# A list scheduler that knows of the port between VectorE and GpSimd

## The chip, the cores and the metric

One core of a Trainium2 chip runs the whole program. The metric is the time of one execution on the device in microseconds (us), the median of three runs. Beside the runs one execution was recorded by the hardware profiler. The engines are TensorE (PE: products; PEld: its weight loads), VectorE (DVE), ScalarE (ACT), GpSimd (POOL) and SyncE (SP), which issues the loads.

## The reference

Two layers over 256 latent tokens and 256 context tokens of 1024 channels, all in float32. Layer 0 mixes tokens by a gated DeltaNet that runs forward and backward, layer 1 by differential attention; a SwiGLU follows each. Every sub-layer is modulated by shift, scale and gate vectors (adaLN) and closed by a LayerNorm.

```
for i in range(DEPTH):                                  # 2
    sh1, sc1, gt1, sh2, sc2, gt2 = split(s_lat @ ada_w[i] + ada_b[i])     # the same for the context
    h, hc = x * (1 + sc1) + sh1, ctx * (1 + sc1c) + sh1c
    y, yc = _gated_deltanet(h, hc, ...) if i == 0 else _diff_attention(h, hc, ...)
    x = _layernorm(DEEPNORM_ALPHA * x + gt1 * y, ln1_g[i], ln1_b[i])
    x = _layernorm(DEEPNORM_ALPHA * x + gt2 * _swiglu(x * (1 + sc2) + sh2, ...), ln2_g[i], ln2_b[i])
    # and the context in the same way, but in the last layer
return x
```

## The kernel before, in words

The order of nearly all instructions is not written by hand. The kernel is a set of generators, called threads: one loads the weights, one splits them, eight groups of nine work through the DeltaNet heads, one (dense_run) goes through the large products, others do the norms, the attention heads and the adaLN vectors. A thread yields operations (Op), each with an engine and an estimated cost, and Sched.run asks each thread when its next operation could start: when its engine is free by the estimates (at), when the thread's last operation has ended plus a delay between the two engines (LAG), and when other engines have left the same PSUM bank. The one that can start first is issued; among equals the thread of the lower rank. An Alt holds the same operation for several engines, and the one that would end first is taken, where spare adds a delay to VectorE's bid. So the estimates decide two things: the order on every engine's own queue, which the hardware then keeps, and which engine an Alt goes to. On the chip the instructions wait for each other by semaphores; the estimates are no longer used there.

TensorE's products take float32 operands as two parts of a narrower type, hi and lo, and mm3 adds three products of them. For the weights ScalarE casts the hi part (wh, wxh, wyh) and VectorE or GpSimd subtracts it from the weight, which gives the lo part (wl, wxl, wyl; lo_op, split). In stage A below lo_op goes to GpSimd unless that is later by 1e6 ns, afterwards by 1e3 ns. The activations' parts are hh and hl, those of the hidden channels hidh and hidl or h1h and h1l; q and k of attention are split into qs, ks and kl after a rotation (rope) that uses rs.

Where TensorE is idle by the estimates for at least 1000 ns, warm inserts products of the tile ones that nobody reads: one for each 216 ns of the wait but its last 600. In the profile they are the line L514 of before, and in what follows they are called fillers.

The stages in the order of time:

- A: the heads of the DeltaNet. Projections (pj), convolution (acc, cv), the inverse of a triangular matrix on small tiles (t) by VectorE, the scan, and the first part of the out-projection. The lo parts here, a sum of each convolution and the decay masks (PQ, EG) are on GpSimd.
- B: the rest of the out-projection, and the first norm (n, bst; sm holds its small vectors, rsqrt is a chain of small VectorE operations on them).
- C: SwiGLU of layer 0 (wgu, wd). Beside it VectorE sums adaLN vectors of later stages (adaE, ada_dve), which TensorE then transposes in the midst of the products.
- D: attention of layer 1. A head's output is normed by another rsqrt chain and ends in ao, which TensorE transposes.
- E: the last norm ahead of SwiGLU of layer 1, that SwiGLU, and the output's norm.

The norms' rows are scaled on GpSimd too (lnr; ln_x), as is in part the split of their results (hl).

Of the kernel before, what the change touches and what calls it, by code (L numbers as in the profile page):

```python
# [17 lines left out]
P = 128  # L18
# [8 lines left out]
# columns of the constants' array  # L27
# [22 lines left out]
def last(ap, n):  # L50
    """[P, a] -> [P, a, n], each value repeated."""
    return ap.unsqueeze(2).to_broadcast([ap.shape[0], ap.shape[1], n])


def mid(ap, n):
    """[P, b] -> [P, n, b], the row repeated."""
    return ap.unsqueeze(1).to_broadcast([ap.shape[0], n, ap.shape[1]])
# [17 lines left out]
# numbers of buffers  # L75
# [40 lines left out]
# The kernel is written as threads of operations. Each step issues the operation that can start first by an  # L116
# estimate of the engines' times; among equals, that of the thread with the lower rank. A thread's operations
# follow each other; threads meet at events and at the buffers they allocate and free.
class Op:
    __slots__ = ("eng", "cost", "fn", "wait", "banks")  # L120

    def __init__(self, eng, cost, fn, *aps):
        self.eng, self.cost, self.fn = eng, cost, fn
        # engines take turns at a bank of PSUM
        self.banks = {a.tensor.name for a in aps if a.space == PSUM}
        self.wait = 0.0     # the delay that is accepted to leave this engine to others


class Alt(list):
    """the same operation on several engines; the one that ends first is taken"""  # L130


class Par(list):
    """operations that do not depend on each other"""
# [10 lines left out]
class Tag:  # L145
    """buffers of one size. Tags of other types may share them; without a pool, a tag only counts"""
# [20 lines left out]
class Alloc:  # L167
    def __init__(self, *tags):
        # (a list may grow while the thread waits)
# [18 lines left out]
class Buf:  # L188
    """an allocated buffer; t is the tile"""
# [21 lines left out]
class Sched:  # L211
    # from the end of an operation to the start of another one that needs it
# [7 lines left out]
    def __init__(self):  # L220
        self.at = {"pe": 0.0, "v": 0.0, "s": 0.0, "g": 0.0, "dma": 0.0}
        self.threads = []
        self.banks = {}
        self.now = 0.0
# [16 lines left out]
    def advance(self, th):  # L241
        """run the thread to its next operation"""
# [47 lines left out]
    def start(self, th):  # L290
        """(start, end, operation) of the thread's next operation, or None while it waits"""
# [8 lines left out]
        for op in it if isinstance(it, Alt) else (it,):  # L300
            s = max(self.at[op.eng], base + self.lag(eng, op.eng))
            for b in op.banks:
# [7 lines left out]
    def run(self, until=None):  # L310
        while self.threads and not (until is not None and until.time is not None):
# [17 lines left out]
            if op.eng != "pe":  # L329
                # an operation of a lower rank that is about to come is worth a short wait  # L330
# [14 lines left out]
            self.at[op.eng] = e  # L345
            for b in op.banks:
                self.banks.setdefault(b, {})[op.eng] = e
# [10 lines left out]
def trunk_kernel(ctx: ExitStack, tc: tile.TileContext, A: dict, out: bass.AP, dbg=None, stop=None):  # L358
# [10 lines left out]
    # ------------------------------------------------------------ operations with their estimated cost  # L369
# [16 lines left out]

    def tt(o, a, b, op, e="v"):
        return Op(e, cost(e, o, (a, b)), lambda: E[e].tensor_tensor(o, a, b, op), o, a, b)  # L388
# [4 lines left out]
    def ts(o, a, s1, s2, o0, o1=None, e="v"):  # L393
        f = lambda: E[e].tensor_scalar(o, a, s1, s2, o0, o1) if o1 is not None else E[e].tensor_scalar(o, a, s1, s2, o0)  # L394
        return Op(e, cost(e, o, (a,), (s1, s2), True), f, o, a)

    def stt(o, a, s, b, o0, o1):
        return Op("v", cost("v", o, (a, b), (s,)), lambda: V.scalar_tensor_tensor(o, a, s, b, o0, o1), o, a, b)  # L398

    def cp(o, a, e="s"):  # L400
        if e == "s":
            return Op("s", cost("s", o, (a,)), lambda: S.copy(o, a), o, a)  # L402
        return Op(e, cost(e, o, (a,), (), True), lambda: E[e].tensor_copy(o, a), o, a)
# [13 lines left out]
    def spare(alt, wait):  # L417
        """leaves DVE free unless the others are later by this much"""
# [8 lines left out]
    def mm(o, l, r, start=True, stop=True):  # L427
        n, m = fs(r), fs(l)
        if l.dtype == F32R:
            c = max(n, 256) / 2.4 + 2  # L430
# [15 lines left out]
    def mm3(o, l, r, start, stop):  # L446
        """the three products of (hi, lo) operands that float32 accuracy needs"""
# [6 lines left out]
    # ranks: a lower one goes first  # L454
# [6 lines left out]
    # ------------------------------------------------------------ buffers of the whole run  # L461
    PS = {k: Tag(ps, [P, 512], F32, k, n) for k, n in (("pj", 2), ("wa", 2), ("wb", 1), ("wc", 2), ("o", 1))}
    YP = [PS[k] for k in ("wb", "wc", "o")]
    # weights: as they come, and their two parts
# [39 lines left out]
    def warm(a, b):  # L504
        """keeps TensorE's clock up while it waits from a to b: products that nobody reads, in a free bank"""
# [20 lines left out]
    def prep_s():  # L526
# [8 lines left out]
        # selB[:, r, :]: ones in the rows 32 g + r  # L535
# [4 lines left out]
    def rsqrt(x, n):  # L540
        """1/sqrt(x[:, :n]), x positive: a first guess from the bits, then two steps. Frees nothing of x"""
# [7 lines left out]
        # 8/3 of a step of third order, then one of second order  # L549
# [10 lines left out]
    # ------------------------------------------------------------ weights  # L560
    pieces = []   # (kind, key, source) in the order of their use
# [28 lines left out]
    def split(raw, n, hi, lo, e, loaded):  # L590
        """the part that float32r holds, and the rest"""
# [15 lines left out]
    def unit(w, i):  # L607
        """i-th quarter (512 columns) of the halves of a piece"""
# [7 lines left out]
    # ------------------------------------------------------------ adaLN vectors  # L616
    def ada_mm(l, v, hf, tag):
        """s @ W of 512 columns, in four row groups that remain to be summed"""
# [16 lines left out]
    def ada_mod_post(l, v, hf, pt):  # L635
        """mods[:, 4 hf.., r] = (s @ W + b [+ 1]) with channels on partitions; r = 0 latent, 1 context"""
# [27 lines left out]
    def ada_dve(l, v, hf, streams, post):  # L664
        """s @ W of 512 columns by DVE, the rows' products remain to be summed over the partitions"""
# [38 lines left out]
    def gate_out(l, v, hf, parts):  # L704
        """the gates, broadcast over the partitions: sums of rows that lhs selects"""
# [35 lines left out]
    # ================================================================= layer 0: gated DeltaNet  # L741
# [48 lines left out]
    # ---- decay and write gates of all heads  # L790
# [1396 lines left out]
```

## Time and profile before

| | before |
|---|---|
| runs, us | 1452.04, 1455.54, 1456.51; median 1455.54 |
| span of the profiled execution, us | 1456.0 |
| PE busy, us | 1282.4 (88%) |
| weight loads busy, us | 1044.1 (72%) |
| DVE busy, us | 1044.6 (72%) |
| ACT busy, us | 578.5 (40%) |
| POOL busy, us | 505.7 (35%) |
| mean granted clock of TensorE | 0.945 |
| DMA | 171.48 MB, 118 GB/s in the mean |

The profiled execution has no time of its own in the list; its span lies within the three runs. Busy time of an engine is the sum of its instructions' durations, and an instruction that stands on its engine waiting for something other than a semaphore counts as busy. The granted clock is the share of full speed that TensorE's throttle let through. Times within a stage are in us from the span's start.

### The profile page before, as it was taken

To read this page: it belongs to the slowest core of one execution; us is meant where nothing else is said; L and a number is where in the kernel's file an instruction comes from. 1 tells how busy PE (TensorE), PEld (TensorE's weight loads), DVE (VectorE), ACT (ScalarE), POOL (GpSimd) and SP (SyncE) were. 2 spreads that over 40 slices of the span, in tenths; PEclk is the share of its full clock that TensorE was granted. 3 is DMA by queue.
4 is the path that set the end of the run, shared out by engine and by line. 5 is a ranking of instruction groups with operands and counts; after the bars stand their busy time and mean duration, and the time that the engine had idled before them with its cause. 6 is when DMAs were issued, how large, how long until landed. Compare 5 with 4: busy or idle time off the path is not lost. (4 is left out here: it accounts for less than half of the span.)

```text
span 1456.0 us, 22451 instructions
## 1 busy us (share of the span) xinstructions
PE 1282.4 (88%) x8606; PEld 1044.1 (72%) x8606; DVE 1044.6 (72%) x2212; ACT 578.5 (40%) x1244; POOL 505.7 (35%) x315
## 2 busy tenths in 40 slices
PE   9977798786888987898999999998889978799997
PEld 6555566565667576877888777877777766799986
DVE  3488989989888558799448664256788878855546
ACT  2364565555553423322221222125445433444432
POOL 1166534445443144524211223226343332422200
PEclk9988999899899998999999999998899989899999
DMA  6524220100111342354425544221332224455551
GB/s 239 203 72 137 96 88 30 44 30 30 38 37 45 117 167 94 116 198 138 157 82 194 189 158 147 84 91 59 137 124 86 88 80 158 163 187 187 185 193 43
DMA packets 47196, 171.48 MB, mean 118 GB/s; under 512 B 5360, under 2 KB 5488, under 8 KB 46320
## 3 DMA queue, kind: packets, MB, share of 16 engines
q1 hardware_dynamic: 47088, 170.04, 34.0%
q8 instruction: 67, 1.10, 0.3%
q14 instruction: 41, 0.34, 0.1%
HBM read 168.97 MB, written 1.05 MB: 117 GB/s over the span
## 5 line engine op out<-in xcount | busy, mean ns | idle before, releaser
L437 PE MATMUL pj<-hl,wh 128*128 128x512 f32 (+1 forms) x648 | 239.7, 370 | 5.6 <-DVE hl L388 5.6
L437 PE MATMUL pj<-hh,wh 128*128 128x512 f32 (+1 forms) x648 | 239.0, 369 | 5.0 <-DVE w L398 1.8
L402 ACT CAST wh<-w 128x1024 fp32r<-128x1024 f32 (+1 forms) x136 | 141.7, 1047 | 224.8 <-PE wa L437 54.2
L388 POOL TENSOR_TENSOR wl<-w,wh 128x1024 fp32r<-128x1024 f32 (+1 forms) x53 | 130.2, 2459 | 266.9 <-ACT wh L402 242.0
L437 PE MATMUL pj<-hh,wl 128*128 128x512 f32 (+1 forms) x512 | 198.8, 388 | 0.0
L437 PEld LDWEIGHTS pj<-hh,wh 128*128 128x128 f32 x648 | 129.0, 199 | 22.2 <-issue 3.0
L437 PEld LDWEIGHTS pj<-hl,wh 128*128 128x128 f32 x648 | 128.7, 199 | 19.4 <-DVE hl L388 4.9
L398 DVE SCALAR_TENSOR_TENSOR adaE<-w,sT,adaE 128x512 f32<-128x512 f32 x112 | 110.8, 1023 | 10.1 <-DMA w<-in_adaw_dram 9.4
L388 DVE TENSOR_TENSOR t<-t,t 128x8 f32<-128x8 f32 (+14 forms) x240 | 114.1, 476 | 4.6
L437 PEld LDWEIGHTS pj<-hh,wl 128*128 128x128 f32 x512 | 102.4, 200 | 12.4
L437 PE MATMUL wa<-hh,wh 128*128 128x256 f32 (+2 forms) x312 | 102.7, 329 | 0.0
L437 PE MATMUL wa<-hl,wh 128*128 128x256 f32 (+2 forms) x312 | 102.7, 329 | 0.0
L388 DVE TENSOR_TENSOR wl<-w,wh 128x1024 fp32r<-128x1024 f32 x44 | 54.3, 1234 | 54.7 <-ACT wh L402 50.9
L388 POOL TENSOR_TENSOR acc<-acc,cv 128x508 f32<-128x508 f32 x48 | 64.2, 1341 | 53.2 <-ACT cv L415 50.2
L388 POOL TENSOR_TENSOR wxl<-w,wh 128x1024 fp32r<-128x1024 f32 x16 | 39.6, 2477 | 102.5 <-ACT wh L402 65.8
L388 POOL TENSOR_TENSOR h1l<-fth,h1h 128x256 fp32r<-128x256 f32 x22 | 32.1, 1457 | 99.2 <-ACT h1h L402 99.2
L437 PE MATMUL pj<-hh,wxl 128*128 128x256 f32 (+1 forms) x200 | 65.0, 325 | 0.0
L437 PEld LDWEIGHTS wa<-hh,wh 128*128 128x128 f32 (+1 forms) x312 | 60.3, 193 | 5.5
L437 PEld LDWEIGHTS wa<-hl,wh 128*128 128x128 f32 (+1 forms) x312 | 60.0, 192 | 5.5
L437 PE MATMUL wa<-hh,wxl 128*128 128x512 f32 (+1 forms) x176 | 61.6, 350 | 0.0
L437 PE MATMUL wa<-hh,wl 128*128 128x256 f32 (+2 forms) x176 | 58.0, 330 | 0.0
L402 ACT CAST wxh<-w 128x1024 fp32r<-128x1024 f32 x29 | 30.3, 1049 | 59.8 <-PE wa L437 21.4
(645 smaller groups left out, 3416.1 us busy)
## 6 DMA issues: line engine op xcount, KB each, us to landing
w<-in_adaw_dram SPq DMA_DIRECT2D x89, 512.0 KB, 4.3
w<-in_wgu_dram SPq DMA_DIRECT2D x64, 512.0 KB, 4.6
w<-in_wd_dram SPq DMA_DIRECT2D x36, 512.0 KB, 4.0
w<-in_wdn_dram SPq DMA_DIRECT2D x26, 512.0 KB, 3.7
wx<-in_wgu_dram SPq DMA_DIRECT2D x22, 512.0 KB, 4.8
w<-in_wo_dram SPq DMA_DIRECT2D x15, 512.0 KB, 3.8
w<-in_wqk_dram SPq DMA_DIRECT2D x12, 512.0 KB, 3.8
lnr<-in_lnr_dram SPq DMA_DIRECT2D x4, 1024.0 KB, 7.8
```

Source lines behind the costliest of these rows:

```text
L388: return Op(e, cost(e, o, (a, b)), lambda: E[e].tensor_tensor(o, a, b, op), o, a, b)
L398: return Op("v", cost("v", o, (a, b), (s,)), lambda: V.scalar_tensor_tensor(o, a, s, b, o0, o1), o, a, b)
L402: return Op("s", cost("s", o, (a,)), lambda: S.copy(o, a), o, a)
L437: return Op("pe", c, lambda: T.matmul(o, lhsT=l, rhs=r, start=start, stop=stop), o)
```

## The change

An Op gets a mark, port. It is set for every operation on GpSimd, and for one on VectorE when no source is in PSUM and it has two sources or writes to SBUF. The scheduler keeps for each of the two engines when its last marked operation ends, and lets a marked operation start, by the estimates, no earlier than the other engine's last one ends. Operations that are given as dve(...) (shuffles, transposes, reductions, statistics) are not marked. The estimate for a product of split operands goes from 1/2.4 ns a column plus 2 to 0.433 ns a column plus 8. Comments and docstrings go too, and the numbers of lines shift (L388 becomes L400, L437 L449, L441 L453, L514 L526).

```diff
 class Op:
-    __slots__ = ("eng", "cost", "fn", "wait", "banks")
+    __slots__ = ("eng", "cost", "fn", "wait", "banks", "port")
...
+        self.port = False
 class Sched:
...
+        self.port = {"v": 0.0, "g": 0.0}
     def start(self, th):
...
             s = max(self.at[op.eng], base + self.lag(eng, op.eng))
+            if op.port:
+                s = max(s, self.port["g" if op.eng == "v" else "v"])
     def run(self, until=None):
...
             self.at[op.eng] = e
+            if op.port:
+                self.port[op.eng] = e
...
+    def shared(op, srcs, out=None):
+        op.port = op.eng == "g" or (op.eng == "v" and not isps(*srcs) and (len(srcs) > 1 or not isps(out)))
+        return op
     def tt(o, a, b, op, e="v"):
-        return Op(e, cost(e, o, (a, b)), lambda: E[e].tensor_tensor(o, a, b, op), o, a, b)
+        return shared(Op(e, cost(e, o, (a, b)), lambda: E[e].tensor_tensor(o, a, b, op), o, a, b), (a, b))
...
     def mm(o, l, r, start=True, stop=True):
         n, m = fs(r), fs(l)
         if l.dtype == F32R:
-            c = max(n, 256) / 2.4 + 2
+            c = max(n, 256) * 0.433 + 8
```

The functions ts, stt and cp get shared(...) in the same way as tt. No operation, tile or load is added or taken away but the fillers; every other instruction may move. Counted over the program, TensorE has the same 6907 products and transposes and 117 fillers before, 481 now. GpSimd has 58 lo parts of weights instead of 80, and 20 of the norms' hl instead of 14; of the small operations on kr, qr, kl, qs and al in attention it has 8 instead of 25. What leaves GpSimd is on VectorE. SP issues the same 329 loads.

The first place is the end of attention and the last norm, on TensorE, at the border of D and E. n_11048 and n_11101 are the normed rows of the two latent tiles, pj_11013 an adaLN product, and the products of wh and hh at the end are the first of SwiGLU. Before:

```order
L437 MATMUL pj_11013<-w_10942,sT 32x512 x2
L514 MATMUL wa_11061<-ones 128x128 x3
L441 MATMUL wc_11057<-cst,n_11048 128x128 x4
L441 MATMUL o_11059<-cst,n_11048 128x128 x4
L514 MATMUL pj_11113<-ones 128x128 x9
L441 MATMUL wb_11108<-cst,n_11101 128x128 x4
L441 MATMUL wc_11110<-cst,n_11101 128x128 x4
L437 MATMUL wc_11134<-w5h_11003,selB 128x512
L437 MATMUL wc_11134<-w5l_11004,selB 128x512
L514 MATMUL pj_11158<-ones 128x128 x9
L437 MATMUL pj_11038<-hh,wh_10967 128x256
```

And now, with n_11399 and n_11469 for the same two tiles:

```order
L449 MATMUL pj_11375<-w_11230,sT 32x512 x2
L453 MATMUL o_11419<-cst,n_11399 128x128 x4
L453 MATMUL wb_11421<-cst,n_11399 128x128 x4
L526 MATMUL pj_11477<-ones 128x128 x49
L453 MATMUL wc_11473<-cst,n_11469 128x128 x4
L453 MATMUL wc_11475<-cst,n_11469 128x128 x4
L449 MATMUL o_11533<-w5h_11457,selB 128x512
L449 MATMUL o_11533<-w5l_11458,selB 128x512
L526 MATMUL pj_11555<-ones 128x128 x17
L449 MATMUL pj_11396<-hh,wh_11329 128x256
```

Between the two tiles stand 49 fillers instead of 9, ahead of SwiGLU's first product 17 instead of 9, and the three ahead of the first tile are gone.

The second place is GpSimd's queue in the middle of attention, where the fifth and sixth head are rotated and split; wl is a lo part of a weight. Before:

```order
L388 TENSOR_TENSOR rs_9814<-rs_9814,rtab 128x256
L388 TENSOR_TENSOR wl_10133<-w_10002,wh_10033 128x1024
L388 TENSOR_TENSOR rs_10175<-rs_10175,rtab 128x256
L388 TENSOR_TENSOR kr_10130<-kr_10130,rtab 128x256
L388 TENSOR_TENSOR rs_10191<-rs_10191,rtab 128x256
L388 TENSOR_TENSOR qs_6_10227<-qr_10171,qs_6_10227 64x256
L388 TENSOR_TENSOR al<-ao_10278,ah 128x256
L388 TENSOR_TENSOR rs_10319<-rs_10319,rtab 128x256
```

And now, a little later in the same stage:

```order
L400 TENSOR_TENSOR rs_10389<-rs_10389,rtab 128x256
L400 TENSOR_TENSOR rs_10428<-rs_10428,rtab 128x256
L400 TENSOR_TENSOR rs_10717<-rs_10717,rtab 128x256
L400 TENSOR_TENSOR rs_10747<-rs_10747,rtab 128x256
L400 TENSOR_TENSOR rs_10795<-rs_10795,rtab 128x256
L400 TENSOR_TENSOR rs_10830<-rs_10830,rtab 128x256
L400 TENSOR_TENSOR wxl_10971<-w_10750,wh_10955 128x1024
```

Only the product of the rotation, which has no other engine, is left of the heads' work, and the next lo part of a weight stands behind the last head's.

The third place is TensorE in C, where the transposes of two adaLN vectors (adaE) stand among the products of SwiGLU. Before:

```order
L437 MATMUL pj_6580<-hl,wh_6414 128x512
L441 MATMUL wc_6607<-cst,adaE_6446 128x128 x4
L437 MATMUL pj_6580<-hh,wxl_6443 128x512
L437 MATMUL pj_6580<-hh,wh_6414 128x512
L437 MATMUL pj_6580<-hl,wh_6414 128x512
L437 MATMUL pj_6580<-hh,wxl_6443 128x512
L437 MATMUL pj_6580<-hh,wh_6414 128x512
L437 MATMUL pj_6580<-hl,wh_6414 128x512
L441 MATMUL wc_6617<-cst,adaE_6475 128x128 x4
```

And now:

```order
L449 MATMUL pj_6935<-hl,wh_6807 128x512
L453 MATMUL wc_6965<-cst,adaE_6791 128x128 x4
L449 MATMUL pj_6935<-hh,wl_6808 128x512
L449 MATMUL pj_6935<-hh,wh_6807 128x512
L449 MATMUL pj_6935<-hl,wh_6807 128x512
L449 MATMUL pj_6935<-hh,wl_6808 128x512
L449 MATMUL pj_6935<-hh,wh_6807 128x512
L453 MATMUL o_6975<-cst,adaE_6816 128x128 x4
```

The pair stands among the products of another chunk of hidden channels: counted from the program's first product, the first of the two comes after 1478 wide products instead of 1427.

More of the change, by code (lines that the diff above doesn't have):

```diff
@@ L126, in __init__ @@
         self.wait = 0.0
+        self.port = False
 class Alt(list):
+    pass
 class Par(list):
+    pass
 class Event:
@@ L394, in ts @@
         f = lambda: E[e].tensor_scalar(o, a, s1, s2, o0, o1) if o1 is not None else E[e].tensor_scalar(o, a, s1, s2, o0)
-        return Op(e, cost(e, o, (a,), (s1, s2), True), f, o, a)
+        return shared(Op(e, cost(e, o, (a,), (s1, s2), True), f, o, a), (a,), o)
     def stt(o, a, s, b, o0, o1):
-        return Op("v", cost("v", o, (a, b), (s,)), lambda: V.scalar_tensor_tensor(o, a, s, b, o0, o1), o, a, b)
+        return shared(Op("v", cost("v", o, (a, b), (s,)), lambda: V.scalar_tensor_tensor(o, a, s, b, o0, o1), o, a, b), (a, b))
     def cp(o, a, e="s"):
@@ L402, in cp @@
             return Op("s", cost("s", o, (a,)), lambda: S.copy(o, a), o, a)
-        return Op(e, cost(e, o, (a,), (), True), lambda: E[e].tensor_copy(o, a), o, a)
+        return shared(Op(e, cost(e, o, (a,), (), True), lambda: E[e].tensor_copy(o, a), o, a), (a,), o)
     def cpa(o, a):
```

## The prediction

> **What bounds the kernel now.** I read the page first: its span, the engines' shares, and the chain that ended last.
>
> ```profile
> span 1456.0 us, 22451 instructions
> ...
> PE 1282.4 (88%) x8606; PEld 1044.1 (72%) x8606; DVE 1044.6 (72%) x2212; ACT 578.5 (40%) x1244; POOL 505.7 (35%) x315
> ...
> PE 12%; DVE 1%; issue 0%; DVEq 0%
> ```
>
> TensorE (PE) is busy 88%, and the chain holds nearly nothing but PE, but it was only followed back through the last 13% of the span. So the next view is the busy time by stage. The stages, in time: A the DeltaNet heads with their projections, B the rest of the out-projection, C the first SwiGLU, D attention, E the second SwiGLU.
>
> ```profile
> 0.00:540.00 540.00, 449.29 (x4002) 332.96 (x4003) 421.88 (x1181) 262.61 (x720) 228.00 (x154) 0.93 0.26 90
> 540.00:571.00 31.00, 26.77 (x117) 21.90 (x116) 27.45 (x58) 8.63 (x21) 10.17 (x6) 0.91 0.39 135
> 571.00:980.00 409.00, 383.49 (x1763) 316.03 (x1763) 262.00 (x337) 105.29 (x141) 121.75 (x61) 0.98 0.41 140
> 980.00:1235.00 255.00, 222.11 (x1281) 182.69 (x1279) 200.12 (x449) 111.89 (x234) 96.41 (x66) 0.91 0.30 101
> 1235.00:1456.00 221.00, 200.71 (x1456) 190.56 (x1448) 133.13 (x190) 90.04 (x130) 49.39 (x31) 0.96 0.47 162
> ```
>
> The columns are the stretch, its length, busy time of PE, weight load, VectorE (DVE), ACT and GpSimd (POOL), then the granted clock and the DMA share. PE stands idle 540 - 449 = 91 us in A, 4 in B, 26 in C, 33 in D and 20 in E: 174 us is all that a better order can win from waits. In A the second-busiest engine is DVE, and its busy time contains waiting, as the time line shows at the last norm of D and E:
>
> ```profile
> 1241.24 2.35 POOL L388 TENSOR_TENSOR big<-n,lnr 128x1024 f32<-128x1024 f32 x1 [2.99 <-DVE sm L394]
> 1241.39 2.22 DVE L388 TENSOR_TENSOR sm<-sm 128x1 f32<-128x1 f32 x1
> 1243.64 0.16 DVE L388 TENSOR_TENSOR sm<-sm,sm 128x1 f32<-128x1 f32 x1
> ```
>
> A product of one column takes DVE 0.16 us, but 2.22 us when GpSimd has begun a 2.35 us operation just before; it ends with GpSimd's. An operation that reads PSUM is not caught: here w<-wc takes its 0.68 us inside GpSimd's pair, and the next one, from SBUF, is caught again.
>
> ```profile
> 1233.17 5.08 POOL L388 TENSOR_TENSOR wl<-w,wh 128x1024 fp32r<-128x1024 f32 x2 [11.19 <-ACT wh L402]
> ...
> 1235.89 0.68 DVE L388 TENSOR_TENSOR w<-wc,gate 128x512 f32<-128x512 f32 x1
> 1236.49 1.77 DVE L388 TENSOR_TENSOR sm<-sm 128x1 f32<-128x1 f32 x1
> ```
>
> The planner of before knows nothing of this, so wherever DVE and GpSimd meet, it believes that DVE's result is there earlier than it is, and puts a TensorE instruction that needs it too early in PE's stream, where it holds all behind it.
>
> **The change, part by part.** First the product estimate. Two rows give the true spacing of products:
>
> ```profile
> 1286.74 2.86 PE pj L437 x24
> ...
> 1384.28 0.69 PE wb L437 x3
> ```
>
> 2.86 / 24 = 119 ns for 256 columns and 0.69 / 3 = 230 ns for 512. The old rule gives 108.7 and 215.3, the new one 118.8 and 229.7: it is right to 1 ns. The products themselves are the same 6907; this edit costs nothing by itself.
>
> Second, the hold. It shifts three things that the order of instructions shows.
>
> (1) Splits leave GpSimd. The weights' low parts are 80 on GpSimd before and 58 after; 17 of 25 small rotary and split operations of attention leave it too. The rows:
>
> ```profile
> L388 POOL TENSOR_TENSOR wl<-w,wh 128x1024 fp32r<-128x1024 f32 (+1 forms) x53 | 130.2, 2459 | 266.9 <-ACT wh L402 242.0
> L388 DVE TENSOR_TENSOR wl<-w,wh 128x1024 fp32r<-128x1024 f32 x44 | 54.3, 1234 | 54.7 <-ACT wh L402 50.9
> L388 POOL TENSOR_TENSOR rs<-rs,rtab 128x256 f32<-128x256 f32 x16 | 14.9, 936 | 31.5 <-DVE rs L1686 18.5 <-issue 6.5 <-DVE sm L388 4.3
> ```
>
> GpSimd loses 22 x 2.46 = 54 us and about 17 x 0.94 = 16 us, DVE gains 22 x 1.23 = 27 us and some 17 x 0.45 = 8 us. In C and D DVE has the room (262 of 409 and 200 of 255, caught time included).
>
> (2) What waits in PE's stream. In attention a head's norm is a chain of small DVE products, caught by a split:
>
> ```profile
> 1177.54 2.33 POOL L388 TENSOR_TENSOR wl<-wx,wh 128x1024 fp32r<-128x1024 f32 x1
> ...
> PE o L441 <- DVE ao L388: 13.1, 5, 7.0
> ...
> PE wa L437 <- POOL qs L388: 5.3, 2, 4.1
> PE wb L437 <- POOL qs L388: 1.6, 1, 1.6
> ```
>
> The last three rows are the waits of PE in D. In the new order GpSimd's queue holds two splits instead of six while the heads run, and 3 instead of 7 of the qs operations for which PE waited 6.9 us. Ends: all of these 20.0 us and a third of the other 13 us idle gained (-24), or +10 if the 35 us of work that DVE takes over come to lie in the same chains. I take -18, near the first end, because the two causes named by the rows are what leaves.
>
> In C the waits of PE are on the adaLN vectors that DVE sums:
>
> ```profile
> L398 DVE SCALAR_TENSOR_TENSOR adaE<-w,sT,adaE 128x512 f32<-128x512 f32 x112 | 110.8, 1023 | 10.1 <-DMA w<-in_adaw_dram 9.4
> ...
> PE wc L441 <- DVE adaE L398: 8.6, 4, 3.2
> PE o L441 <- DVE adaE L398: 2.9, 3, 1.5
> PE wb L441 <- DVE adaE L398: 2.6, 1, 2.6
> ...
> L398 DVE SCALAR_TENSOR_TENSOR adaE<-w,sT,adaE x100: 736/746/2902, 602.9 to 894.7; 128x512 f32<-128x512 f32 x100
> ```
>
> PE waits 14.1 us there. Twelve such groups of transposes stand in C. In the new stream four of them come 50 to 57 products later, and eight lie between 17 products earlier and 9 later. Fewer splits on GpSimd also shorten the chain itself, whose links take 746 ns in the median and up to 2902 (the last row: least, median, most). Ends: -14, and +6 if three of the earlier ones stand 17 x 0.119 = 2.0 us longer; I take -8, about half of the wait, for the four moved ones and the shorter chain. B stays at 0: its 4 us idle bound it.
>
> In A the splits stay (34 and 31), and so does nearly everything else: 22 of 1050 DVE operations go to ACT. How much DVE is caught there, two groups of the same 15 shapes on the same tiles tell:
>
> ```profile
> L388 DVE TENSOR_TENSOR t<-t,t 128x8 f32<-128x8 f32 (+14 forms) x240 | 114.1, 476 | 4.6
> ...
> L1078 DVE STREAM_SHUFFLE t<-t 128x8 f32<-128x8 f32 (+14 forms) x120 | 28.1, 234 | 0.2
> ```
>
> The product reads two tiles and means 476 ns, the shuffle one and 234: 240 x 0.24 = 58 us caught in this group alone. But the hold moves no time out of GpSimd in A; it can only bring DVE's PSUM operations under GpSimd's. With 228 us of GpSimd and DVE busy 422 of 540, most of that is taken. Ends: -58 (this group freed) and +25 (a quarter of PE's 91 us added by a worse interleaving); I take -12, the end nearest to no change, since the same work shares the same port.
>
> At the three norms GpSimd takes more, not less: 20 of the low halves (hl) instead of 14.
>
> ```profile
> L388 POOL TENSOR_TENSOR hl<-w,hh 128x512 fp32r<-128x512 f32 x14 | 18.4, 1315 | 50.2 <-ACT hh L402 36.2 <-DVE hh L403 7.0 <-DVE sm L398 6.5
> ```
>
> Each is 1.3 us where half a split on DVE is 1234 / 2 = 0.6, and at E's norm two of them now stand in GpSimd's queue behind a 2.35 us product with lnr. PE waits for hl there. Ends: 0, and 3 x 2.35 + 6 x 0.7 = +11; I take +3, one third, since two of the three norms have other products for PE.
>
> (3) Fillers. Where the planner sees PE idle for 1 us or more it puts in products that nobody reads (L514). There are 117 before and 481 after: 80 to 280 in A, 12 to 74 in B and at the first norm, 4 to 61 in D with the norm ahead of it, 21 to 66 in E.
>
> ```profile
> 23.08 6.42 PE L514 MATMUL pj<-ones 128*128 128x128 f32 x56
> ...
> 1242.44 3.33 PE L514 MATMUL pj<-ones 128*128 128x128 f32 x18
> ```
>
> Each is two records, so 6.42 / 28 = 0.229 us at full clock, and 364 more are 83 us of PE. Where the wait is real they cost nothing; their cover is a late DVE result. At the norm of E the cover can be read: 9 fillers start at 1242.44 and the next tile's transposes at 1246.22, 3.8 us, where 49 now stand, 11.2 us: up to 7.4 us too many, unless the norm has become that slow. Ends: 0, and +42 (half of them uncovered). I take +7: 4 at this norm and 3 in all other places, near the first end, as PE's 174 us of idle are twice the fillers' time.
>
> (4) The clock. Fillers also keep PE from standing. What standing does to it:
>
> ```profile
> 1255.00:1261.50 6.50, 5.42 (x26) 5.15 (x26) 6.50 (x6) 2.27 (x3) 0.85 (x1) 0.51 0.45 142
> 1262.00:1280.00 18.00, 18.00 (x152) 17.91 (x151) 9.86 (x13) 7.14 (x11) 4.15 (x3) 1.00 0.77 269
> ```
>
> After the waits at the norm 26 products take 5.42 us at a granted clock of 0.51, and then 152 take 18.00. By the five stage rows the clock lost is 0.07 x 540 + 0.09 x 31 + 0.02 x 409 + 0.09 x 255 + 0.04 x 221 = 80 us, most of it while PE stands anyway. Ends: 0 and -40 (half of it); I take -7.
>
> [...]
>
> The loads are the same 329 in SP's queue, some rows of x and of the gates behind other weights than before; with DMA engines at 0.26 to 0.47 they cost 0.
>
> The sum: -12 (A) -8 (C) -18 (D) +3 (norms) +7 (fillers) -7 (clock) = -35. From the profiled execution's span of 1456.0 us, which lies 0.5 above the median of the runs (1455.54) with nothing to add around it, that is 1421 us.
>
> **The rivals.** *The fillers hold PE up* (slower). In PE's stream they stand ahead of products that E and C need at once, and the planner places them by waits that it believes in now as firmly as it did not before. Without the fillers' term the sum is -42. If more than 42 of the 83 us are uncovered, it is slower; at 60 us, 1456 - 42 + 60 = 1474. For it: the 11.2 us where 3.8 were needed. Against it: PE idles longer than the fillers last in A (91 against 46 us) and D (33 against 13).
>
> *The clock stays up and the heads come free* (much faster). With the clock at its -40 end and a third of the 58 us caught in A: 1421 - 33 - 7 = 1381. Against it: A's work on the port is the same.
>
> *The order makes no difference*. DVE, with GpSimd's time in it, sets A, and the products set C and E, so what is won in D is lost at the fillers: 1456. For it: PE busy 200 of 221 and 383 of 409 in E and C.
>
> **How the numbers follow.** A difference of 0.3%, 4.4 us, is about what a measurement of this kernel can tell. The forecast, 1385 to 1445, has 0.48; much faster 0.12; no difference, 1445 to 1462, 0.11; the fillers, 1462 to 1490, 0.29. Faster by over 4.4 us are the first two and a little of the third: 0.62; the same 0.09; slower 0.29. The range leaves about 0.1 on each side: 1380 to 1475.
>
> **What would show it.** In the new profile: no PE wait on ao above 3 us in D, and POOL busy near 440 us instead of 506; the DVE group t<-t,t still near 450 ns; fillers busy for 110 us; the clock of A at 0.95 or more. I am wrong if A becomes longer than 540 us, or if waits of other engines on the fillers or products right behind a burst show that their operands had been there before it began.

## The result and the profile after

The changed kernel takes 1406.82 us (median of 4 runs, 1406.49 to 1407.65) against 1456.03 of the kernel before in the same comparison: a ratio of 0.9665, with a 95% interval of 0.9642 to 0.9688. That is 49 us less where 35 were forecast, inside the range.

From the page of the changed kernel, the span, the engines and the chain that ended last:

```profile
span 1405.9 us, 23922 instructions
...
PE 1324.4 (94%) x9334; PEld 1102.9 (78%) x9334; DVE 968.9 (69%) x2215; ACT 590.1 (42%) x1274; POOL 435.1 (31%) x282
...
PE 65%; DVE 24%; ACT 5%; DMA 3%; issue 3%; POOL 0%; DVEq 0%; ACTq 0%; POOLq 0%; SPq 0%
```

GpSimd lost 71 us (505.7 to 435.1), VectorE 76 us (1044.6 to 968.9). PE is busy longer, since it holds 364 more fillers. The chain now reaches back through the whole program, and GpSimd's share of it is 0%.

Stages are compared best at a place that both programs have. I cut at the first transpose of a normed row (cst,n) of each of the three norms: the first stretch is the heads and most of the out-projection (A), then SwiGLU with the rest of B ahead of it (C), attention (D), and the last norm with the second SwiGLU (E). The columns are those of the stage rows in the prediction. Before:

```profile
0.00:557.00 557.00, 466.29 (x4075) 346.79 (x4076) 436.56 (x1212) 263.33 (x721) 230.41 (x155) 0.94 0.27 93
557.00:974.20 417.20, 387.46 (x1775) 319.15 (x1774) 270.61 (x352) 108.85 (x150) 127.25 (x63) 0.97 0.41 139
974.20:1241.10 266.90, 229.32 (x1317) 188.46 (x1317) 210.34 (x472) 117.57 (x247) 101.93 (x68) 0.91 0.31 105
1241.10:1456.00 214.90, 199.31 (x1442) 189.74 (x1442) 127.07 (x178) 88.71 (x129) 46.14 (x29) 0.96 0.46 156
```

After:

```profile
0.00:548.50 548.50, 504.07 (x4490) 392.13 (x4490) 388.32 (x1190) 271.02 (x746) 213.40 (x149) 0.96 0.27 96
548.50:948.40 399.90, 388.80 (x1883) 324.67 (x1883) 259.96 (x364) 110.64 (x150) 102.73 (x54) 0.99 0.42 144
948.40:1189.10 240.70, 225.67 (x1428) 189.02 (x1427) 205.56 (x495) 118.58 (x250) 62.02 (x44) 0.98 0.34 118
1189.10:1406.00 216.90, 205.90 (x1536) 197.04 (x1536) 115.07 (x168) 89.90 (x130) 56.99 (x35) 0.98 0.44 154
```

So A gives 8.5 us, C 17.3, D 26.2, and E costs 2. In D GpSimd is busy 62 us instead of 102, and TensorE's waits there read, in the list of waits of the changed kernel for 948.4 to 1189.1:

```profile
PE o L453 <- DVE sm L406: 5.6, 1, 5.6
PE wc L453 <- DVE n L406: 2.6, 1, 2.6
PE wb L453 <- DVE n L406: 2.2, 1, 2.2
...
PE o L453 <- DVE ao L400: 0.5, 1, 0.5
```

Of the 13.1 us behind ao 0.5 are left, and the 6.9 us behind GpSimd's qs are gone. What is left is mostly waits for the norms at the two ends of the stretch: the row with sm is the norm behind the attention (at 1189.1), the rows with n are the one ahead of it (at 967.8 and 977.5). In C, 548.5 to 948.4, the waits on adaE are 6.4 us (the rows with adaE) instead of 14.1:

```profile
PE wc L453 <- DVE adaE L410: 3.5, 2, 2.7
PE wc L453 <- ACT n L427: 3.0, 1, 3.0
PE wb L453 <- DVE adaE L410: 1.9, 2, 1.1
PE wb L453 <- DVE n L406: 1.6, 1, 1.6
PE o L453 <- DVE adaE L410: 1.0, 1, 1.0
```

### The profile page after: what moved, and what is told of

The parts are those of the page before. It is cut to its first block, busy times and chain, and to the rows that moved or that the text cites. A ratio compares the mean times of both kernels' runs of the same rounds, so it can differ in the third digit from the quotient of the medians.

```text
span 1405.9 us, 23922 instructions
## 1 busy us (share of the span) xinstructions
PE 1324.4 (94%) x9334; PEld 1102.9 (78%) x9334; DVE 968.9 (69%) x2215; ACT 590.1 (42%) x1274; POOL 435.1 (31%) x282
## 4 chain that ended last, share of the span: by engine, by line
PE 65%; DVE 24%; ACT 5%; DMA 3%; issue 3%; POOL 0%; DVEq 0%; ACTq 0%; POOLq 0%; SPq 0%
PE pj L449 25%; PE wa L449 15%; PE wc L449 8%; PE o L449 6%; PE wb L449 5%; DVE t L400 4%; DMA w<-in_adaw_dram 2%; PE pj L526 2%; DVE adaE L410 2%; DVE sm L406 2%; DVE sm L400 2%; ACT jk L427 1%; DVE wl L400 1%; DVE sm L410 1%; DVE wxl L400 1%
## 5 line engine op out<-in xcount | busy, mean ns | idle before, releaser
L449 PE MATMUL pj<-hh,wh 128*128 128x512 f32 (+1 forms) x608 | 222.6, 366 | 5.3 <-DVE mod_sc L660 3.6
L449 PE MATMUL pj<-hl,wh 128*128 128x512 f32 (+1 forms) x608 | 220.9, 363 | 0.1
L449 PE MATMUL pj<-hh,wl 128*128 128x512 f32 (+1 forms) x400 | 154.4, 386 | 0.4 <-DVE wl L400 0.4
L400 POOL TENSOR_TENSOR wl<-w,wh 128x1024 fp32r<-128x1024 f32 (+1 forms) x38 | 91.3, 2403 | 158.9 <-ACT wh L414 150.5
L449 PEld LDWEIGHTS pj<-hh,wh 128*128 128x128 f32 x608 | 116.6, 192 | 21.7 <-DVE mod_sc L660 3.8
L449 PEld LDWEIGHTS pj<-hl,wh 128*128 128x128 f32 x608 | 116.5, 192 | 14.3 <-issue 0.5
L400 DVE TENSOR_TENSOR wl<-w,wh 128x1024 fp32r<-128x1024 f32 x58 | 72.1, 1245 | 44.8 <-ACT wh L414 41.8
L400 POOL TENSOR_TENSOR acc<-acc,cv 128x508 f32<-128x508 f32 x48 | 63.8, 1332 | 110.8 <-ACT cv L427 90.1
L400 DVE TENSOR_TENSOR t<-t,t 128x8 f32<-128x8 f32 (+14 forms) x240 | 91.5, 381 | 3.2
L410 DVE SCALAR_TENSOR_TENSOR adaE<-w,sT,adaE 128x512 f32<-128x512 f32 x102 | 84.2, 858 | 10.0 <-DMA w<-in_adaw_dram 9.5
L449 PEld LDWEIGHTS pj<-hh,wl 128*128 128x128 f32 x400 | 77.1, 193 | 13.0 <-DVE wl L400 0.8
L449 PE MATMUL pj<-hh,wxl 128*128 128x256 f32 (+1 forms) x264 | 86.5, 328 | 0.0
L449 PE MATMUL wa<-hh,wh 128*128 128x256 f32 (+2 forms) x248 | 82.9, 334 | 0.0
L449 PE MATMUL wa<-hl,wh 128*128 128x256 f32 (+2 forms) x248 | 82.6, 333 | 0.0
L400 POOL TENSOR_TENSOR hidl<-w,hidh 128x512 fp32r<-128x512 f32 x22 | 31.4, 1425 | 137.4 <-ACT hidh L414 137.4
L400 DVE TENSOR_TENSOR wxl<-w,wxh 128x1024 fp32r<-128x1024 f32 x36 | 45.4, 1260 | 38.2 <-ACT wxh L414 38.1
L449 PE MATMUL wa<-hh,wl 128*128 128x256 f32 (+2 forms) x208 | 70.0, 337 | 0.0
L400 DVE TENSOR_TENSOR wxl<-w,wh 128x1024 fp32r<-128x1024 f32 x25 | 35.1, 1403 | 32.8 <-ACT wh L414 31.5
L449 PE MATMUL wa<-hh,wxl 128*128 128x256 f32 (+1 forms) x168 | 54.8, 326 | 0.0
L400 POOL TENSOR_TENSOR h1l<-fth,h1h 128x256 fp32r<-128x256 f32 x22 | 29.4, 1336 | 77.0 <-ACT h1h L414 77.0
```

What stands on the lines that cost most here:

```text
L400: return shared(Op(e, cost(e, o, (a, b)), lambda: E[e].tensor_tensor(o, a, b, op), o, a, b), (a, b))
L410: return shared(Op("v", cost("v", o, (a, b), (s,)), lambda: V.scalar_tensor_tensor(o, a, s, b, o0, o1), o, a, b), (a, b))
L449: return Op("pe", c, lambda: T.matmul(o, lhsT=l, rhs=r, start=start, stop=stop), o)
```

## The experiments

One table has all lengths, cut as above in each kernel's own profile (E by the span); the us of all runs is the median, the ratio is to the kernel before in the same comparison. Lengths of a stage whose order two kernels share mostly agree closely (A is 557.0 and 556.9 in two kernels, 548.5 in three), but est_only and hold_rest, which share the order of A but for its end, differ by 3.0 us there, and a profile as a whole can lie some us off its median (4.7 in est_only). Lo parts in D are those of weights on GpSimd in that stretch.

| kernel | us | ratio, 95% | A | C | D | E | fillers | lo parts in D |
|---|---|---|---|---|---|---|---|---|
| before | 1456 | 1 | 557.0 | 417.2 | 266.9 | 214.9 | 117 | 15 |
| changed | 1406.8 | 0.9665 (0.9642 to 0.9688) | 548.5 | 399.9 | 240.7 | 216.8 | 481 | 8 |
| hold_only | 1402.1 | 0.9627 (0.9603 to 0.9650) | 555.1 | 395.8 | 240.4 | 209.0 | 488 | 8 |
| est_only | 1468.1 | 1.0079 (1.0056 to 1.0102) | 564.4 | 432.9 | 251.1 | 213.3 | 143 | 7 |
| before_nofill | 1454.5 | 0.9987 (0.9974 to 0.9999) | 549.0 | 420.5 | 267.9 | 212.9 | 0 | 15 |
| after_nofill | 1417.8 | 0.9729 (0.9702 to 0.9755) | 553.2 | 402.6 | 246.5 | 216.0 | 0 | 8 |
| bid_only | 1424.4 | 0.9786 (0.9768 to 0.9805) | 561.4 | 402.8 | 243.9 | 214.4 | 165 | 7 |
| start_only | 1434.3 | 0.9854 (0.9835 to 0.9873) | 560.9 | 400.0 | 261.3 | 210.7 | 533 | 17 |
| hold_A | 1453.6 | 0.9966 (0.9946 to 0.9987) | 548.5 | 433.7 | 255.2 | 213.1 | 328 | 11 |
| hold_rest | 1420.7 | 0.9759 (0.9727 to 0.9791) | 561.4 | 399.3 | 241.0 | 217.9 | 276 | 8 |
| before_Dv | 1436.9 | 0.9861 (0.9832 to 0.9890) | 556.9 | 418.1 | 249.7 | 214.5 | 132 | 1 |
| after_Dg | 1422.4 | 0.9756 (0.9728 to 0.9784) | 548.5 | 400.0 | 264.2 | 208.9 | 522 | 33 |
| hold_lw0 | 1400.5 | 0.9608 (0.9579 to 0.9638) | 555.2 | 391.9 | 240.4 | 207.9 | 508 | 1 |
| hold_tiny | 1425.9 | 0.9783 (0.9750 to 0.9816) | 569.8 | 391.3 | 251.1 | 211.6 | 502 | 9 |

**Which of the two edits.** hold_only is the changed kernel with the old price of a product, est_only the kernel before with the new one.

```diff
# hold_only
-            c = max(n, 256) * 0.433 + 8
+            c = max(n, 256) / 2.4 + 2
```

> The changed kernel with the old product estimate (n/2.4 + 2), so the hold alone. Theory 1, the hold makes the gain (49 us) by what it changes in the order: within 10 us of the changed kernel's 1407, so 1400 to 1417. Theory 2, the two estimates count about alike, because TensorE's queue is what they place: half of the gain, 1425 to 1440. Theory 3, any other order of this list would do as well: 1440 to 1456.

> The kernel before with the new product estimate alone. Theory 1, the hold makes the gain: 1445 to 1460 (a right price of products moves the planner's products by 7% later and lets a few more splits go to DVE, worth at most 10 us). Theory 2, both count alike: 1425 to 1440. Theory 3, the product estimate is the cause: 1405 to 1420.

Theory 1 holds for the first: the hold alone gives 54 us, somewhat more than both edits. For the second none holds. The new price alone makes the kernel 12 us slower, which is beyond the expected end: a price that is right to 1 ns moves the order in A (+7.4), C (+15.7) and D (-15.8). In est_only's C the waits for adaE grow to 19.2 us:

```profile
PE wc L441 <- DVE adaE L398: 9.5, 4, 3.1
PE o L441 <- DVE adaE L398: 6.7, 3, 3.5
...
PE wb L441 <- DVE adaE L398: 3.0, 1, 3.0
```

So the hold is worth 54 us on the old price and 61 on the new one. The price costs 12 us without the hold; with it the intervals of hold_only and of the changed kernel overlap. In D alone the new price helps, and it takes splits off GpSimd there: 7 lo parts instead of 15, and 251.1 us instead of 266.9.

**Order or fillers.** In both of these only the fillers are left out. Every other instruction stands where it stood.

```diff
-                for _ in range(n):
+                for _ in range(0):
                     T.matmul(t[:, 0:P], lhsT=ones, rhs=ones, start=True, stop=True)
```

> The kernel before without its 117 fillers (33 us of TensorE); every other instruction stands in the same order on its engine. Theory 1, fillers lie in real waits and do little: 1450 to 1460. Theory 2, fillers hold the clock up: at before's half-clock episodes, 57 us of lost products with 33 us of fillers, 1460 to 1475.

> The changed kernel without its 481 fillers (107 us of TensorE by their spacing); every other instruction stands in the same order on its engine. Theory 1, the gain is from the order and the fillers lie in real waits: 1400 to 1412, and below 1407 if bursts hold back ready products. Theory 2, the gain is from the clock that the fillers hold up (0.976 granted instead of 0.945; half-clock episodes cost 57 us before and 19 now): 1435 to 1450, the loss of 38 us back.

Before, 117 fillers do nothing that can be told clearly (-1.4 us without them). In the profiles A is 8.0 us shorter without them, 6.5 of it in the first 83 us, and C 3.3 longer. After, 481 fillers win 11.0 us, between the two theories: three quarters of the gain is the order (1454.5 to 1417.8, 36.7 us), one quarter the fillers. The stretches of after_nofill, to be held against those of after, show where the clock goes (the granted clock stands behind the five engines, 0.90 instead of 0.96 in A, 0.93 instead of 0.98 in D):

```profile
0.00:553.20 553.20, 457.82 (x3930) 337.57 (x3930) 386.67 (x1190) 271.43 (x746) 214.14 (x149) 0.90 0.28 95
553.20:955.80 402.60, 376.13 (x1735) 311.53 (x1735) 257.72 (x364) 110.80 (x150) 101.88 (x54) 0.97 0.43 143
955.80:1202.30 246.50, 220.25 (x1305) 181.93 (x1305) 204.28 (x495) 118.50 (x250) 61.17 (x44) 0.93 0.34 115
1202.30:1418.30 216.00, 194.81 (x1404) 184.48 (x1404) 116.27 (x168) 89.80 (x130) 56.76 (x35) 0.94 0.46 155
```

But fillers also stand in the way. At the last norm, the time line of the changed kernel's TensorE:

```profile
1189.08 1.09 PE L453 MATMUL o<-cst,n 128*128 128x128 f32 x4 [5.64 <-DVE sm L406]
1189.96 1.06 PE L453 MATMUL wb<-cst,n 128*128 128x128 f32 x4
1190.82 11.62 PE L526 MATMUL pj<-ones 128*128 128x128 f32 x98
1202.27 1.04 PE L453 MATMUL wc<-cst,n 128*128 128x128 f32 x8
...
1207.32 0.36 PE L449 MATMUL pj<-hh,wh 128*128 128x256 f32 x1
```

And the same place of after_nofill:

```profile
1202.33 1.09 PE L453 MATMUL o<-cst,n 128*128 128x128 f32 x4 [5.64 <-DVE sm L406]
1203.21 1.06 PE L453 MATMUL wb<-cst,n 128*128 128x128 f32 x4
1204.68 1.12 PE L453 MATMUL wc<-cst,n 128*128 128x128 f32 x4 [0.42 <-DVE n L406]
1211.65 1.11 PE L453 MATMUL wc<-cst,n 128*128 128x128 f32 x4 [5.84 <-ACT n L427]
...
1214.64 0.58 PE L449 MATMUL pj<-hh,wh 128*128 128x256 f32 x1 [1.03 <-ACT hh L414]
```

From the first transposes to SwiGLU's first product it is 12.3 us without fillers and 18.2 with them. So 5.9 us of fillers are uncovered here: the second tile's rows were there at 1191.4 and 1198.4, and the burst ran to 1202.3. SwiGLU behind them gets most of it back at a better clock (0.98 instead of 0.94): E is 216.8 with and 216.0 without. At the start of the program fillers stand in the way too: the changed kernel's first product stands behind 21 fillers and begins at 9.12 us, without fillers at 5.39; in the kernel before it is 8.34 and 5.54.

**Bids or start times.** The hold enters twice: in the bid that chooses between VectorE and GpSimd, and in the time at which an operation is taken to start. q below is the held start.

```diff
# bid_only
-            if op.port:
-                s = max(s, self.port["g" if op.eng == "v" else "v"])
...
-            if best is None or s + op.cost + op.wait < best[0]:
-                best = (s + op.cost + op.wait, s, s + op.cost, op)
+            q = max(s, self.port["g" if op.eng == "v" else "v"]) if op.port else s
+            if best is None or q + op.cost + op.wait < best[0]:
+                best = (q + op.cost + op.wait, s, s + op.cost, op)
# start_only: the bid by s, the start and the end by q
```

> The changed kernel with the hold only in the choice of an engine for operations that may go to several (the one that would end first, the hold counted), and not in the time at which an operation is taken to start. With the new product estimate the references are 1468 us (no hold) and 1407 (the whole hold). The order then has 53 lo parts of weights and 4 small operations of attention on GpSimd (80 and 25 before, 58 and 8 with the whole hold) but only 165 fillers (117 and 481). Theory 1, the hold wins by taking splits off GpSimd: 1405 to 1425, with 20 us of it lost in the fillers that are missing. Theory 2, it wins by later start times, which put TensorE's instructions later and fill the waits: 1445 to 1468.

> The opposite part: the hold only in the time at which an operation is taken to start, and not in the choice of an engine. The order has 83 lo parts of weights and 28 small operations of attention on GpSimd, as many as before, and 533 fillers. References 1468 us (no hold) and 1407 (the whole hold). Theory 1, the gain is the splits off GpSimd: 1445 to 1465, of which at most 20 us come from fillers. Theory 2, the gain is the later start times: 1405 to 1425.

bid_only comes out as its theory 1 has it, at the upper end (1424 of 1405 to 1425). start_only lies between its two theories: the start times alone win more than the first has and less than the second. So neither cause is the only one: against est_only (1468) the bids give 44 us and the start times 34, both together 61. The table shows where. In C either one gives all of it (402.8 and 400.0 of 432.9 to 399.9): the start times get the transposes of adaE late enough even with 30 lo parts on GpSimd (16 in the changed kernel), and the only wait on adaE left is

```profile
PE o L452 <- DVE adaE L409: 2.4, 1, 2.4
```

The bids alone leave 7.7 us of these waits, by the other way: their first transposes come no later than before, but with 15 lo parts on GpSimd VectorE's 128 adaE operations in C take 830 ns in the mean instead of 979 before and 965 in start_only.

D is otherwise. The bids make it 243.9, the start times alone 261.3, longer than est_only's 251.1. The two differ in the splits too: start_only has 17 lo parts on GpSimd there, est_only 7. With so many the planner knows that the heads are late, and what it does is to fill: start_only has 152 fillers in D (304 records), est_only 5. What the fillers and what the splits cost there isn't told apart by these two runs.

**Which stage.** The planner gets the hold in one part of the program only.

```diff
# hold_A (hold_rest has self.stage > 0)
-            if op.port:
+            if op.port and self.stage == 0:
                 s = max(s, self.port["g" if op.eng == "v" else "v"])
...
+        sched.stage = k
```

> The changed kernel with the hold in the DeltaNet heads' stage alone (A, which is planned by itself); from the first norm on the estimates know nothing of the port. By stages, cut at the same number of products, the kernel with the product estimate alone takes 552, 32, 420, 241 and 217 us, the changed one 528, 38, 388, 228 and 223. If stages add up: 528 + 32 + 420 + 241 + 217 = 1438. Theory 1, most of the gain is behind A (39 of the 56 us): 1430 to 1445. Theory 2, the heads are where the port is crowded and the rest follows from where A leaves the engines: under 1420.

> The opposite part: the hold from the first norm on, and the heads planned without it. If stages add up: 552 + 38 + 388 + 228 + 223 = 1429, so theory 1: 1420 to 1437. Theory 2, the heads carry the gain: over 1445.

hold_rest is where theory 1 put it (1421). hold_A gives 15 us against est_only instead of 30, lies outside both of its theories, and misses the sum of stages: A is 548.5 as it should be, but C stays at 433.7 and D becomes 255.2. Its waits for adaE are 21.0 us, as without any hold:

```profile
PE wb L454 <- DVE adaE L411: 9.5, 3, 3.5
PE wc L454 <- DVE adaE L411: 6.9, 2, 4.4
...
PE o L454 <- DVE adaE L411: 4.6, 2, 2.6
```

The medians of the two add up to the whole: 14.6 + 47.4 = 62 of 61 us. The gain is mostly behind the heads.

**The cause in D.** The bonus on VectorE's bid, or the delay, for the weights' lo parts while D is planned:

```diff
# before_Dv
-LO_WAIT = (1e6, 1e3, 1e3, 1e3, 1e3)
+LO_WAIT = (1e6, 1e3, 1e3, -1e6, 1e3)
# after_Dg: 1e6 in the place of -1e6, in the changed kernel
```

> The kernel before, where VectorE's bid for a weight's lo part gets a bonus instead of a delay while attention (D) is planned: no lo part of a weight goes to GpSimd there, 66 in all instead of 80; nothing else is changed by hand, and the estimates know nothing of the port. The small operations of the heads stay on GpSimd (30). Cut at the first transposes of a normed row, D takes 267 us before and 241 in the changed kernel. Theory 1, the splits between GpSimd's operations for the heads are the cause of D's waits: D 243 to 252 and 1432 to 1442 us in all. Theory 2, the splits cost what the start times don't show, so only the hold on start times helps: D over 260, 1450 to 1458.

> The changed kernel with the lo parts of D put back on GpSimd (81 in all instead of 58), the hold and all else kept. Theory 1, the splits on GpSimd are the cause of D's waits: D 255 to 265 instead of 241, 1420 to 1432 in all, with the fillers now counting as uncovered or the waits on ao back. Theory 2, the hold alone keeps operations clear of each other: D 240 to 248, 1405 to 1413.

Both came out as theory 1 has it. Without the hold, only by taking D's splits from GpSimd, the kernel before becomes 20 us faster (1436.9), and D 249.7 instead of 266.9. GpSimd's largest group there is then the rotation's own product:

```profile
L388 POOL TENSOR_TENSOR rs<-rs,rtab 128x256 f32<-128x256 f32 x16 | 16.3, 1019 | 54.4 <-DVE rs L1686 35.0 <-DVE sm L394 9.0 <-issue 7.9
```

And its waits on ao fall from 13.1 to 3.9 us:

```profile
PE o L441 <- DVE ao L388: 3.9, 3, 3.1
```

Put back by force under the hold, 33 lo parts make D 264.2 and the kernel 15.5 us slower than the changed one. The wait on ao does not come back (0.2 us); D's fillers go from 61 to 140, GpSimd's busy time from 62 to 122 us:

```profile
948.50:1212.70 264.20, 246.54 (x1586) 208.12 (x1585) 204.03 (x474) 126.33 (x261) 121.93 (x68) 0.98 0.32 107
```

A reader who looked only at PE's busy time (226 to 247 us) and its waits would think this D better used. How many lo parts there are does not settle D's length alone: with 7 to 9 of them it is 240.4 to 251.1 in the table.

**Two attempts at a better version**, both on hold_only.

```diff
# hold_lw0
-LO_WAIT = (1e6, 1e3, 1e3, 1e3, 1e3)
+LO_WAIT = (1e6, 0, 0, 0, 0)
# hold_tiny: an operation with one source is marked only above 16 columns
-(len(srcs) > 1 or not isps(out)))
+(len(srcs) > 1 or not isps(out)) and (len(srcs) > 1 or fs(srcs[0]) > 16))
```

> The faster of the versions so far (hold alone, 1402 us) without the delay of 1000 ns on VectorE's bid behind A: 32 lo parts on GpSimd, nearly all of them A's, instead of 62. Theory 1, each split that leaves GpSimd behind A helps: D gains little more (2 us), C and E some 2 to 4 each: 1394 to 1400. Theory 2, VectorE becomes the late engine: its busy time in C and D rises by 30 x 1.24 = 37 us, and the transposes and norms wait for it: 1405 to 1420.

> The hold alone, with the mark taken from VectorE's operations with one source of at most 16 columns (tensor_scalar and copies): the trace shows that many of the smallest of these run through while GpSimd is busy (0.15 us). Theory 1, their false hold makes the norms' chains look longer than they are and puts in fillers that are not needed: 1398 to 1401. Theory 2, no difference that can be told: 1401 to 1406.

hold_lw0 is the fastest kernel of all, 1400.45 us (1398.01 to 1401.79): its interval lies below that of the changed kernel, and overlaps that of hold_only, from which it can't be told. C is 3.9 us shorter than hold_only's, D the same though only one lo part is left there: what the splits cost in D was already gone with eight. It ends just outside theory 1 (1400), and VectorE did not become the late engine. hold_tiny missed by 20 us: A is 14.7 us longer than hold_only's, D 10.7, and C 4.5 shorter. Of the chains of small products those with two sources are still caught. At its first norm eight operations of one column and one source (TENSOR_SCALAR) take 0.71 us in all while GpSimd is busy until 579.55. Then three of one column and two sources (TENSOR_TENSOR) take 2.44 us together beside a split of 2.33, and TensorE waits 12.35 us for that normed row (until 583.21):

```profile
577.21 2.34 POOL L400 TENSOR_TENSOR big<-big,lnr 128x1024 f32<-128x1024 f32 x1
579.51 2.33 POOL L400 TENSOR_TENSOR wxl<-w,wh 128x1024 fp32r<-128x1024 f32 x1
...
578.62 0.71 DVE L406 TENSOR_SCALAR sm<-sm 128x1 f32<-128x1 f32 x8
...
579.49 2.44 DVE L400 TENSOR_TENSOR sm<-sm 128x1 f32<-128x1 f32 x3
```

But this place lies in C, the stretch that became shorter, so it does not explain the loss. The limit of 16 columns unmarks too much, though: in the traces of before and after all 19 and 26 TENSOR_SCALAR operations of one source and one column that began inside a GpSimd operation, at least 0.2 us before its end, ran through (0.13 to 0.16 us each), and all 10 and 14 of one source and two or four columns were caught (0.58 to 2.34 us). Of the operations that hold_tiny unmarks, 64 of the 69 in A have four columns, 32 of the 85 in D two, and all 16 in C one. That fits a longer A and D and a shorter C, but not E, which has ten of one column and is 2.6 us longer, and no run unmarks the one-column operations alone, so where the 25 us in A and D come from stays open; est_only shows that a change of estimates can move A by 7 us and C by 16 without a reason that one would name ahead.

## Why the prediction was right, point by point

The direction, the main causes and the range held; the forecast was 14 us short. The sum of the order alone (A, C, D and the norms) was -12 - 8 - 18 + 3 = -35, and the two kernels without fillers measure -36.7 for it. That these agree is in part luck: by the profiles of the two, A is 4.2 longer, C 17.9 and D 21.4 shorter and E 3.1 longer, so the term for A promised 16 us too much, and those for C and D together 13 too little. The terms for the fillers and the clock were +7 and -7. Measured, the fillers and what they do to the clock win 11.0 us after, and 1.4 are lost to them before: -12.4 in all. -36.7 - 12.4 is the result. So the step that was mis-sized in the total is (3) and (4) together, +7 - 7 = 0 where -12.4 was measured, and the term for A is the one whose miss the others hid.

- **Splits leave GpSimd in D (-18).** Right in cause, shown by before_Dv (D -17.2) and after_Dg (D +23.5); the measured D is -26.2, of which 5.8 are fillers by after_nofill's D.
- **adaE in C (-8).** Right place: the waits on adaE fell by 7.7 us (14.1 to 6.4). C as a whole is 17.3 shorter, 2.7 of it by fillers. The rest, some 7 us, is about what the waits for the first norm, at the start of C, lost (n, sm and hl: 10.9 us of the listed waits before, 4.6 after), which the term left out. The prediction gave two reasons, later transposes and a shorter chain. start_only has the first without the second and bid_only the second without the first, and C is about as short in both (400.0 and 402.8).
- **A (-12).** The size came out near (-8.5) by luck; the reasoning did not hold. The prediction said that the group t<-t,t would stay near 450 ns, since the hold moves no work out of GpSimd in A, and made heads that come free a rival's gain. It fell to 381 ns after, but to 392 in est_only too, whose A is 7.4 us longer than before. In the changed kernel:

```profile
L400 DVE TENSOR_TENSOR t<-t,t 128x8 f32<-128x8 f32 (+14 forms) x240 | 91.5, 381 | 3.2
```

  And in est_only:

```profile
L388 DVE TENSOR_TENSOR t<-t,t 128x8 f32<-128x8 f32 (+14 forms) x240 | 94.2, 392 | 4.4
```

  So a VectorE that is caught less does not by itself shorten A. Without fillers A is 4.2 us longer after than before (553.2 and 549.0); the gain of A as measured is in the fillers: by these single profiles those of before cost A 8.0 us and those of after win it 4.7.
- **Norms (+3) and fillers (+7).** At the last norm the prediction had up to 7.4 us of fillers too many and took 4; 5.9 are shown. E is 2 us longer. At the program's start, which the prediction did not look at, the first product comes 3.7 us later behind fillers. On balance they win; how many of the others lie in real waits no run shows.
- **The clock (-7).** Too small. With the same order the mean granted clock is 0.976 with fillers and 0.929 without. Of the -40 end, which was half the clock lost before, the net effect of fillers and clock is 11.
- **The product estimate (0).** Wrong by itself: it costs 12 us without the hold. The products are the same, but the price places them, and this the prediction left out.
- **The rivals.** The fillers do not hold PE up on balance, since leaving them out is slower. The clock's rival fits the last 12 us (0.976 granted with the changed kernel's fillers, 0.929 without), with the heads' part missing. That the order makes no difference is ruled out by after_nofill, which is 36.7 us faster than before_nofill.

Of the signs named beforehand, the wait on ao (0.5 us left of 13.1), GpSimd's 435 us and the clock of A (0.96) came as said, fillers are busy 126 us by the groups instead of 110 (107 by their spacing), and the t group was the one that failed. A, cut as in the prediction, is 528 us and not over 540. The sign against it, operands that were there before a burst began, is not met at the last norm: they came 0.6 and 7.5 us after it had begun, and 10.9 and 3.9 before it ended. At the other bursts it was not read.

In the traces of before and after the clock is granted in full or by half. The stretches at half clock last 3.4 us or a multiple of it but for the last one, and there are 32 before and 11 after. In the 3.4 us ahead of a fall TensorE was busy 0 to 51% before, and 0 to 57% after but for one fall behind 73%; it stood all that time in 3 of the 32 cases of before. So the clock fell behind windows that were half busy too, not only behind standing.

## What to carry to other kernels

A list scheduler should charge the hold between two engines where it chooses between them, not only where it dates the operation: a true date without the choice left the splits on GpSimd and filled attention with 152 products that nobody reads. Before new rules are added, try the coarse lever that the profile points at: forbidding the splits on GpSimd in the one stage whose chains are short and serial gave 20 of the 49 us with one number. And a more exact price for one engine alone can make a plan worse; here it cost 12 us without the hold, and under the hold it won nothing that can be told.

## What the runs showed of the hardware

With the order fixed, 481 fillers raised the mean granted clock from 0.929 to 0.976 and won 11.0 us, although at the last norm 5.9 us of them stood ahead of products that were ready. Before the change 117 fillers moved the time by 1.4 us. That the same instrument is worth nothing in one order and 11 us in another was not expected.

Cut the trace of before into windows of 3.4 us along its stretches of full and half clock, which are multiples of that length but for the last. Its clock fell behind windows in which TensorE was busy 0 to 51%, and stayed full behind windows with 44 to 100%: between 43 and 52% lie four windows ahead of a fall and five behind which it stayed full. All 31 returns to the full clock came behind windows with 88 to 100% (82 to 100% for the 10 of the changed kernel), but three windows with 100% were followed by half clock again. So in this trace waits that were filled in part did keep the clock at times; what shorter bursts would win no run shows.

Beside GpSimd's operations some of VectorE's short operations ended late and others did not. In the traces of before and after take those on at most four columns in SBUF that began inside a TENSOR_TENSOR of GpSimd, at least 0.2 us before its end. All with two sources (TENSOR_TENSOR), 20 before and 15 after, took 0.25 to 2.37 us and ended 0.01 to 0.02 us behind it. Of those with one source (TENSOR_SCALAR) all of two or four columns, 10 and 14, did so too (0.58 to 2.34 us, ending 0.03 us behind it), and all of one column, 19 and 26, ran through in 0.13 to 0.16 us. The mark port does not know of the last case.
